# FFN operands made name by name in the text's order, with two and three plain pairs a layer

## The chip, the cores and the metric

The kernel runs on one core of one Trainium2 chip. The metric is the device time of one execution in microseconds, as the median of the runs shown. Engines are named TensorE (PE, with its weight loads as PEld), VectorE (DVE), ScalarE (ACT), GpSimd (POOL) and SyncE (SP, which only issues loads).

## The reference, cut to what matters

A two-layer trunk of 512 tokens and 1024 channels in float32. Each layer is a token mixer (dilated attention in layer 0, causal pooling in layer 1) followed by a gated FFN of width 2816, each behind an RMS norm and with a residual add:

```python
def rmsnorm(x, g):
    y = x * lax.rsqrt(jnp.mean(x * x, axis=-1, keepdims=True) + RMS_EPS)
    return y * g

def swiglu_ffn(h, w_gate_up, w_down):
    gu = h @ w_gate_up
    gate, up = gu[..., :D_FF], gu[..., D_FF:]
    return (jax.nn.silu(gate) * up) @ w_down

for i in range(DEPTH):                       # DEPTH = 2
    x = x + mixer[i](rmsnorm(x, mixer_norm[i]))
    x = x + swiglu_ffn(rmsnorm(x, ffn_norm[i]), w_gate_up[i], w_down[i])
return rmsnorm(x, final_norm)
```

## The kernel before, in words

Activations lie transposed: eight tiles X[k] of 128 channels by 512 tokens. Every matrix product is done in three TensorE passes, because each float32 operand is split into a high part (rounded, by ScalarE) and a low part (the rest, by VectorE): weight high by data high, weight high by data low, weight low by data high. The helper `split` does that for any tile.

**The FFN.** Its 2816 hidden channels are 22 tiles of 128; a pair j is the gate and the up column of one tile. There are two ways to compute a pair.

- A plain pair is two products of 8 x 3 matmuls of 512 columns, made from X scaled by the norm's weights only (`scaled`, the tiles `held[op, k]`). The norm's factor per token (`row`) is not yet needed; VectorE multiplies the result by `row` later. The first pairs of a layer are plain, and they run while the norm is still being computed. Their weights are "lean": ScalarE writes the high part and its negative, and a DMA issued by GpSimd adds the weights from memory to the negative, so VectorE has no part in it.
- A block pair (`strassen_pair`, `chained`) multiplies 2 x 2 blocks by the Strassen-Winograd scheme: seven block products of 4 x 3 matmuls of 256 columns. They are called, in the order of the code, 11, 1, 2, 21, 3, 22, 4. Each name needs an operand T[name, k] from the normed X: sums and differences of its quarters, split into high and low. Three accumulators in PSUM are used several times: alpha takes 11, 2, 3, 4, gamma takes 1 and 22, beta takes 21. Between two uses of an accumulator ScalarE copies it out (lines 535, 539, 543, 551), and the next block product of that accumulator adds on top. The weights of a block pair are made in four steps, `blocks`, `sums`, `more`, `last` (weight tiles b, s, m, l); b serves 11 and 21, s serves 1 and 3, m serves 2 and 22, l serves 4.

Before, `NPLAIN = 4`: four plain pairs in each layer, and `prepare(k)` makes all names of one k beside each of them (line 1108). PARTS says how the hidden tiles are used: pairs 0 and 1 go into plain down products, 2 to 17 into two runs of block down products, 18 to 21 into plain ones.

**The norm ahead of the FFN.** `note` scales a finished X tile and adds its square to a sum. `rstd` sums over channels on TensorE (line 411), VectorE adds epsilon (414), GpSimd raises to -1/2 (417); `spread` brings the result into a row on TensorE (424), ScalarE copies it (430). Before, two products run on seven of eight k ahead of this, the third product is cut in half around `spread`, and five products follow the row.

**The order of work.** The program is written once in text. A scheduler then orders each engine's instructions by the text's priority and by what it takes to be ready, and puts the semaphores. Weights come through rings of five 1024-wide tiles (`w`), two half-wide ones and four raw ones; `pump` is called behind every product and does the next load or weight step when its ring slot is free. `after` in `chained` is a table of hooks: functions that are run in the text behind block product 0 to 6. PSUM has eight banks. Scaled tiles, names, hidden tiles and temporaries share slots: NEAR and SLOTS lie in two large tiles, OPEN are loose.

The steps of a block product, its copy and its hooks:

```python
        mult(alpha, wb, 0, T, "11", n)
        nc.scalar.copy(a, alpha)
        behind(0)
        mult(gamma, ws, 0, T, "1", n)
        nc.scalar.copy(d, gamma)
        behind(1)
        mult(alpha, wm, 0, T, "2", n, on=True)
```

Of the kernel before, what the change touches and what calls it, by code (L numbers as in the profile page):

```python
# [8 lines left out]
F32 = mybir.dt.float32  # L9
F32R = mybir.dt.float32r  # L10
AF = mybir.ActivationFunctionType
OP = mybir.AluOpType
# [38 lines left out]
NEAR = 11  # L51
OPEN = 2
FIXED = NEAR + OPEN
# [12 lines left out]
def trunk(ctx: ExitStack, tc: tile.TileContext, xT, xN, norms, w_first, w_qk, w_qkp, w_v0, w_v0p, w_v12, w_out, w_outp, w_pair, w_down, w_dblock, w_pin, w_pgrp,  # L66
# [134 lines left out]

    turn = [0]

    def pump(n=1, must=False):

        turn[0] += not must
        for i in range(n):
            while loads and all(free(r, c) for r, c in loads[0][1].items()):
                loads[0][0].issued = turn[0]
                loads.popleft()[2]()  # L210
            if not steps or not free(steps[0][1]):
                assert not must
                return
            unit, back = steps[0][0], BACK.get(steps[0][2].__name__)
            if not must and back and unit.back and turn[0] < unit.issued + back:
                return
            steps.popleft()[2]()

    def pairs(*srcs, shift=LINE // 4, back=False):
# [39 lines left out]
    def ffn_plan(layer):  # L259
        j = 0  # L260
        for i, (first, end, block) in enumerate(PARTS):
            while j < min(max(end + block, NPLAIN), FC):
                if j < NPLAIN:
                    plain_gu(layer, j)
                else:
                    pairs(w_pair[layer, j], shift=0, back=True)
                j += 1
            if block:
# [32 lines left out]
    class Product:  # L301


        def __init__(self, n, ins, w=None, keep=None):
            self.n, self.ins, self.done, self.p, self.w = n, ins, 0, ps(), w
            self.sizes = units_of(n)
            self.tiles, self.keep = keep or [], keep is not None
# [10 lines left out]
        def add(self, ks, cols=slice(0, S), pos=None):  # L318
            for k in ks:
                if self.w:  # L320
                    w, c = self.w, k if pos is None else pos + k
                else:
                    held, c = self.where(k)
                    w = held.t
                    if c == self.sizes[len(self.tiles) - 1] - 1 and not self.keep:
                        held.done()
# [52 lines left out]

    def square(layer, k, engine=None):  # L380
        sq = tmp.tile([P, S], F32, name="sq", bufs=3)
        nc.scalar.activation(sq, X[k], AF.Square)
        if layer in acc:
            (engine or nc.vector).tensor_add(sq, acc[layer], sq)
        acc[layer] = sq

    def scaled(layer, k, hi, lo, on_dve=False):
# [7 lines left out]
        operand[layer, k] = hi, lo  # L395

    def note(layer, k):

        if layer < 4:
            held[layer, k], t = slot("h", open=layer == 2 and k == KC - 1)  # L400
            scaled(layer, k, t[:, 0], t[:, 1])
        square(layer, k)
# [197 lines left out]
    with tc.tile_pool(name="opool", bufs=1) as opool:  # L600
        early = [opool.tile([P, 2, S], F32R, tag=f"o{k}", name="early") for k in range(K2)]
        with tc.tile_pool(name="apool", bufs=1) as apool:
# [285 lines left out]
            def halve(h):  # L888

                if h < 3:  # L890
                    OP2[h] = tuple(apool.tile([P, S], F32R, tag=f"qk{h}{c}", name="oh") for c in range(2))
                else:
                    held["o", h], b = slot("oh", open=h == 3)
                    OP2[h] = b[:, 0], b[:, 1]
                split(*OP2[h], o[h])
# [155 lines left out]

            def residual(m, p):
                x = X[m].rearrange("p (q c r) -> p q c r", c=NT, r=NT)
                nc.vector.tensor_add(x, x, p.rearrange("p (r c q) -> p q c r", r=NT, c=NT))
                note(1, m)

            for m in range(NOUT):
                residual(m, lead.pop(0).add([last]).p)
            for u in range(2):
                one, two = (apool.tile([P, S], F32, tag=tag, name="one") for tag in ("s0", "s12"))  # L1060
                seven(T2, one, two, scratch)
                if u:
                    for k in range(2):
                        give(("s", k))
                for c, p in enumerate((one, two)):
                    residual(NOUT + 2 * u + c, p)
# [3 lines left out]
            residual(KC - 1, f.p)  # L1070

    with tc.tile_pool(name="fpool", bufs=2) as fpool:
# [13 lines left out]
        def ffn(layer, nxt, lead, row):  # L1086
# [3 lines left out]
            def gu():  # L1090
                return lead.pop(0).p if lead else product(op)

            def plain_pair(j, up):
                pg = gu()
                gt = ftile("gt")
                nc.vector.tensor_mul(gt, pg, row)
                prepare(j)
                pu = gu()
                if j == NPLAIN - 1:
                    for k in range(KC):  # L1100
                        give((op, k))
                nc.vector.tensor_mul(up, pu, row)
                nc.scalar.activation(gt, gt, AF.Silu)
                nc.vector.tensor_mul(up, up, gt)

            T = {}

            def prepare(k):


                h, t = normed(op, k, row, Temp(), Temp(), True)
                hq, b22 = h.t.rearrange("p (a b c) -> p a b c", a=2, b=2), h.t[:, 3 * H2:]
                held["t", k, 0], b = slot("tb", apart=True)
                split(b[:, 0].rearrange("p (a c) -> p a c", a=2), b[:, 1].rearrange("p (a c) -> p a c", a=2), hq[:, :, 0])
                T["11", k], T["21", k] = (tuple(b[:, e, i * H2:(i + 1) * H2] for e in range(2)) for i in range(2))
                for i, names in enumerate((("1", "2"), ("3", "4"))):
                    held["t", k, 1 + i], b = slot("tt", apart=True)
                    split(b[:, 0], b[:, 1], t.t[:, i * S:(i + 1) * S])
                    for a, name in enumerate(names):
                        T[name, k] = tuple(b[:, e, a * H2:(a + 1) * H2] for e in range(2))  # L1120
                if k % 2 == 0:
                    held["t", k, 3], T["n"] = slot("tn", apart=True)
                n = tuple(T["n"][:, e, k % 2 * H2:(k % 2 + 1) * H2] for e in range(2))
                split_neg(*n, b22)
                T["22", k] = n
                h.done()
                t.done()

            B, U, late = {}, {}, deque()

# [43 lines left out]
            def strassen_pair(u, first=None, right=None):  # L1174
                gt = ftile("gt")
                hooks = waiting()
                if "keep" in U:
# [7 lines left out]
                if first:  # L1185
                    hooks.setdefault(2, []).extend([later(give, ("t", k, 1)) for k in range(K2)] + [first])
                if right:
# [8 lines left out]
            def gate_up(j, ahead):  # L1196
                first, block = next((p[0], p[2]) for p in PARTS if p[0] <= j < p[1])
                u = tmp.tile([P, S], F32, tag="sq", name="u", bufs=3) if block or ahead else ftile("up")
                i, odd = (j - first) // 2, j % 2
                if j < NPLAIN:  # L1200
                    plain_pair(j, u)
                elif block and odd and j == FC - 1:
                    strassen_pair(u, later(operands, i, U["even"]), later(operands_right, i, u))
# [7 lines left out]
                elif not block:  # L1211
                    if NPLAIN <= j < FC - 1:
                        U["keep"] = j, u
# [13 lines left out]

            j = 0
            for first, end, block in PARTS:
                while j < min(max(end + block, NPLAIN), FC):  # L1230
                    gate_up(j, block and j == end)
                    j += 1
                last = end == FC
# [28 lines left out]

        lead = begin(2, 1, range(KC - 1))
        row = finish(lead, 1, [KC - 1])
        ffn(0, 2, lead, row)
# [11 lines left out]
        lead = begin(2, 2, range(KC - 2))  # L1277
        row = finish(lead, 2, range(KC - 2, KC))
        Y = {}
# [38 lines left out]
        def mix(g):  # L1318
            if g not in M:
                mixed(g)  # L1320
            for c, f in enumerate(M.pop(g)):
                m = 2 * g + c
                nc.vector.scalar_tensor_tensor(X[m], f.p, nrm[:, 5, m:m + 1], X[m],
                                               op0=OP.mult, op1=OP.add)
                held[3, m], t = slot("n")
                scaled(3, m, t[:, 0], t[:, 1])
            for c in range(2):
                square(3, 2 * g + c)
                give(("y", g, c))

        pool(3)
# [7 lines left out]
        mix(1)  # L1339
        lead = begin(2, 3, range(4, KC))  # L1340
        mix(0)
        for key in [key for key in held if key[0] == "wg"]:
            give(key)
        for f in lead:
            f.add(range(2, 4))
        row = finish(lead, 3, range(2))
        hidden, HALF = ffn(1, 4, lead, row)


# [177 lines left out]
```

## Time and profile before

| what | value |
|---|---|
| median of 3 runs | 1186.02 us (1185.07 to 1186.65) |
| span of the profiled execution | 1184.0 us |
| what lies between that span and the median | 2.0 us |
| TensorE busy in the span | 1175.4 us (99%) |
| VectorE busy | 989.0 us (84%) |
| ScalarE busy | 721.7 us (61%) |
| GpSimd busy | 171.3 us (14%) |

The span runs from the first to the last instruction of one execution on the chip. An engine's busy time leaves out its waits. TensorE's matmuls overlap one another, so the distance between the starts of two matmuls, not the length of one, is what a matmul costs. The first FFN's norm ends at about 482 us of the span, the second one's at about 864.

### The profile page before, as it was taken

The numbers are of one execution on the slowest core, as the hardware profiler recorded it, in microseconds if no ns is written. First come the engines' busy times: TensorE is split into PE (matmuls) and PEld (weight loads), VectorE is DVE, ScalarE is ACT, GpSimd is POOL, SyncE is SP. The second block draws the span as 40 slices with busy tenths as digits, with TensorE's granted clock in tenths as the row PEclk, the third lists the DMA queues.
The fourth block names the chain that finished last, engine by engine and source line by source line (L and its number), as shares of the span: only waits on it lengthen the run. The fifth ranks groups of instructions, "written<-read, shape, count | busy, mean of one in ns | idle before, by whom it ended". The sixth has DMA issues, their size and how long they took to land.

```text
span 1184.0 us, 25180 instructions
## 1 busy us (share of the span) xinstructions
PE 1175.4 (99%) x10042; PEld 1119.9 (95%) x10042; DVE 989.0 (84%) x1733; ACT 721.7 (61%) x1262; POOL 171.3 (14%) x165
## 2 busy tenths in 40 slices
PE   9999999999999999999999999999999999999997
PEld 7889999999999989889999999988889999999997
DVE  7997898889789888699988988656789998898875
ACT  6554564546455557747756775775575766676553
POOL 1101111111111002311111111122130111111100
PEclk9999999999999999999999999999999999999999
DMA  8537667666856557957777877798595777877732
GB/s 302 130 95 187 147 153 166 168 160 152 192 140 169 145 157 195 246 113 203 191 188 189 204 184 209 195 265 208 121 195 119 187 199 195 198 191 193 197 92 72
DMA packets 83766, 207.57 MB, mean 175 GB/s; under 512 B 7856, under 2 KB 13120, under 8 KB 83648
## 3 DMA queue, kind: packets, MB, share of 16 engines
q1 hardware_dynamic: 52672, 144.84, 36.9%
q0 software_dynamic: 30688, 60.83, 31.6%
q8 instruction: 78, 1.28, 0.4%
q14 instruction: 40, 0.33, 0.1%
q10 hardware_dynamic: 288, 0.29, 0.1%
HBM read 203.84 MB, written 2.10 MB: 174 GB/s over the span
## 4 chain that ended last, share of the span: by engine, by line
PE 96%; DMA 1%; issue 1%; DVE 1%; ACT 0%; POOL 0%; POOLq 0%; DVEq 0%; ACTq 0%
PE ps L461 21%; PE ps L462 20%; PE ps L463 20%; PE ps L329 7%; PE ps L330 7%; PE ps L332 7%; PE ps L928 2%; PE ps L632 2%; PE ps L633 2%; PE ps L634 2%; DMA raw<-w_outp 1%; PE ps L847 1%; PE ps L716 1%; PE ps L736 1%; PE ps L841 1%
## 5 line engine op out<-in xcount | busy, mean ns | idle before, releaser
L92 ACT ACTIVATE w<-raw 128x1024 fp32r<-128x1024 f32 x268 | 283.7, 1063 | 177.0 <-PE ps L463 73.3
L93 DVE TENSOR_TENSOR w<-raw,w 128x1024 fp32r<-128x1024 f32 x268 | 326.4, 1222 | 48.8 <-ACT w L92 44.7
L461 PE MATMUL ps<-far,w 128*128 128x256 f32 x896 | 246.5, 275 | 0.0
L462 PE MATMUL ps<-far,w 128*128 128x256 f32 x896 | 246.4, 275 | 0.0
L463 PE MATMUL ps<-far,w 128*128 128x256 f32 x896 | 246.4, 275 | 0.0
L461 PE MATMUL ps<-near,w 128*128 128x256 f32 x676 | 190.5, 282 | 0.0
L462 PE MATMUL ps<-near,w 128*128 128x256 f32 x676 | 186.9, 277 | 0.0
L463 PE MATMUL ps<-near,w 128*128 128x256 f32 x676 | 186.9, 276 | 0.0
L462 PEld LDWEIGHTS ps<-far,w 128*128 128x128 f32 x896 | 168.2, 188 | 0.1
L461 PEld LDWEIGHTS ps<-far,w 128*128 128x128 f32 x896 | 168.2, 188 | 0.1
L463 PEld LDWEIGHTS ps<-far,w 128*128 128x128 f32 x896 | 168.2, 188 | 0.0
L461 PEld LDWEIGHTS ps<-near,w 128*128 128x128 f32 x676 | 127.1, 188 | 0.5
L462 PEld LDWEIGHTS ps<-near,w 128*128 128x128 f32 x676 | 127.1, 188 | 0.0
L463 PEld LDWEIGHTS ps<-near,w 128*128 128x128 f32 x676 | 127.0, 188 | 0.0
L329 PE MATMUL ps<-near,w 128*128 128x512 f32 (+1 forms) x316 | 119.4, 379 | 0.0
L332 PE MATMUL ps<-near,w 128*128 128x512 f32 (+1 forms) x316 | 118.7, 376 | 0.0
L330 PE MATMUL ps<-near,w 128*128 128x512 f32 (+1 forms) x316 | 118.7, 376 | 0.0
L173 POOL DMA_DIRECT2D raw<-w_pair x36 | 43.6, 1210 | 291.7 <-DMA raw<-w_pair 87.3
L329 PEld LDWEIGHTS ps<-near,w 128*128 128x128 f32 x316 | 59.3, 188 | 11.0 <-ACT near L92 0.4
L332 PEld LDWEIGHTS ps<-near,w 128*128 128x128 f32 x316 | 59.3, 188 | 10.9
L330 PEld LDWEIGHTS ps<-near,w 128*128 128x128 f32 x316 | 59.4, 188 | 10.6 <-DVE near L93 0.2
L92 ACT ACTIVATE half<-rawhalf 128x512 fp32r<-128x512 f32 x84 | 52.8, 630 | 13.7 <-PE ps L463 11.8
(333 smaller groups left out, 2802.7 us busy)
## 6 DMA issues: line engine op xcount, KB each, us to landing
raw<-w_pair SPq DMA_DIRECT2D x80, 512.0 KB, 4.9
raw<-w_qkp SPq DMA_DIRECT2D x38, 512.0 KB, 4.5
raw<-w_pair POOLq DMA_DIRECT2D x36, 512.0 KB, 7.6
raw<-w_dblock SPq DMA_DIRECT2D x32, 512.0 KB, 4.7
raw<-w_qkp POOLq DMA_DIRECT2D x19, 512.0 KB, 7.5
raw<-w_v SPq DMA_DIRECT2D x18, 512.0 KB, 4.1
rawhalf<-w_pair SPq DMA_DIRECT2D x36, 256.0 KB, 5.2
raw<-w_dblock POOLq DMA_DIRECT2D x16, 512.0 KB, 7.5
```

The source lines that it names most:

```text
L92: nc.scalar.activation(hi, v, AF.Copy)
L93: nc.vector.tensor_tensor(lo, v, hi.bitcast(F32), op=OP.subtract)
L173: nc.gpsimd.dma_start(self.b.rearrange("p (a c) -> p a c", a=2), self.src[:, None, 3 * n:].to_broadcast([P, 2, n]), accum_op=OP.add)
L329: nc.tensor.matmul(self.p[:, cols], w[0][:, s], mh[:, cols], start=self.done == 0, stop=False)
L330: nc.tensor.matmul(self.p[:, cols], w[0][:, s], ml[:, cols], start=False, stop=False)
L332: nc.tensor.matmul(self.p[:, cols], w[1][:, s], mh[:, cols], start=False, stop=self.done == self.n)
L461: nc.tensor.matmul(dst, w.t[0][:, c], th, start=k == 0 and not on, stop=False, skip_group_check=on)
L462: nc.tensor.matmul(dst, w.t[0][:, c], tl, start=False, stop=False, skip_group_check=on)
L463: nc.tensor.matmul(dst, w.t[1][:, c], th, start=False, stop=k == n - 1, skip_group_check=on)
L632: nc.tensor.matmul(o, mh, wh, start=k == 0, stop=False)
L633: nc.tensor.matmul(o, mh, wl, start=False, stop=False)
L634: nc.tensor.matmul(o, ml, wh, start=False, stop=k == K2 - 1)
```

## The change

- `NPLAIN = (2, 3)`: two plain pairs in layer 0, three in layer 1. Pairs 2 and 3 (layer 0) and 3 (layer 1) are block pairs now. The down weights of the first part come behind two block pairs (AHEAD).
- The names of the block pairs are made one name at a time for all k, in five stages of the generator `prepared`. The stages are written between the plain products, and the last (name 4) behind the first block product.
- `until` makes weight steps at fixed places of the text; `hold` and `barred` keep `pump` from making others there.
- The plain results are left in PSUM. They are scaled, gated and split in the hooks of the first block pair (`scaled_next`, `kept`), not beside their products; Silu works in place on PSUM.
- `finish` takes the norm's sum earlier: in layer 0 half a product stands ahead of it and half between the sum and `spread`; three products follow. In layer 1 two products stand around it, and four follow.
- The last X tiles ahead of the norm are scaled after their squares, not before.
- From the last attention block product pair (layer 0) or the last pooling group (layer 1) to the end of the second block pair VectorE and ScalarE run in the order of the text (`tc.manual_schedule(engines=BY_HAND)`).
- NEAR goes from 11 to 9, OPEN from 2 to 4; a product gives its weights back when all its columns were used, in any order.

The diff, cut to its core:

```diff
-NPLAIN = 4
+NPLAIN = (2, 3)
+AHEAD = 2
+BY_HAND = {mybir.EngineType.DVE, mybir.EngineType.Activation}
-NEAR = 11
-OPEN = 2
+NEAR = 9
+OPEN = 4
...
-            if not steps or not free(steps[0][1]):
+            if not steps or not free(steps[0][1]) or ((hold[0] or steps[0][0] in barred) and not must):
...
+    def until(what):
+        done = False
+        while not done:
+            while loads and all(free(r, c) for r, c in loads[0][1].items()):
+                loads[0][0].issued = turn[0]
+                loads.popleft()[2]()
...
+            unit, ring, f = steps.popleft()
+            done = what in (f.__name__, unit)
+            f()
...
-    def finish(lead, layer, ks):
-        for f in lead:
-            f.add(ks)
+    def finish(lead, layer, now, behind, rest=()):
+        for f, ks in now:
+            f.add(ks)
+        hold[0] = bool(behind)
         r = rstd([acc[layer]])
-        lead += begin(1, layer, range(4))
+        for f, ks in behind:
+            f.add(ks)
+        if behind:
+            until(barred[layer // 2])
+            if layer == 1:
+                until("blocks")
+        else:
+            lead += begin(1, layer, range(4))
+            rest = [(lead[-1], range(4, KC))]
         row = row_of(spread(r))
-        lead[-1].add(range(4, KC))
+        for f, ks in rest:
+            f.add(ks)
...
+            grown(KC - 1, f.p)
+            noted(1, KC - 3)
+            square(1, KC - 1)
+            for k in (KC - 2, KC - 1):
+                noted(1, k)
...
+            def scaled_pair(j):
+                gt, pu = gu(), gu()
+                up = tmp.tile([P, S], F32, tag="sq", name="u", bufs=3) if j > 1 else ftile("up")
+                nc.vector.tensor_mul(gt, gt, row)
                 nc.vector.tensor_mul(up, pu, row)
                 nc.scalar.activation(gt, gt, AF.Silu)
...
+                normed(0)
+                each(lambda p: named("11", p, a(p, 0)))
+                each(lambda p: nc.vector.tensor_sub(a(p, 0), a(p, 1), a(p, 0)))
+                each(lambda p: named("1", p, a(p, 0)))
+                yield
+                normed(1)
+                each(lambda p: nc.vector.tensor_sub(a(p, 0), a(p, 0), d(p, 1)))
+                each(lambda p: named("2", p, a(p, 0)))
+                yield
+                each(lambda p: named("21", p, d(p, 0)))
+                each(lambda p: nc.vector.tensor_sub(a(p, 1), d(p, 1), a(p, 1)))
+                each(lambda p: named("3", p, a(p, 1)))
+                yield
+                each(lambda p: named("22", p, d(p, 1), split_neg))
+                yield
+                each(lambda p: nc.vector.scalar_tensor_tensor(d(p, 0), a(p, 0), -1.0, d(p, 0), op0=OP.mult, op1=OP.subtract))
+                each(lambda p: named("4", p, d(p, 0)))
...
+            next(stage)
+            upto(2 * plains - 2)
+            until("sums")
+            upto(2 * plains - 1)
+            next(stage)
+            until("more")
+            next(stage)
+            until("last")
+            upto(2 * plains)
+            until("blocks")
+            next(stage)
...
+            j = plains
+            beginning.update({0: [lambda: next(stage)], 1: [later(until, "sums")], 2: [scaled_next] * (plains - 2),
+                              3: [later(until, "more"), scaled_next], 4: [scaled_next], 5: [kept], 6: [free_again]})
...
+                    if j == plains + 1:
+                        ordered.__exit__(None, None, None)
...
-        lead = begin(2, 1, range(KC - 1))
-        row = finish(lead, 1, [KC - 1])
+        lead = begin(1, 1, range(K2))
+        row = finish(lead, 1, [], [(lead[0], range(K2, KC))], [])
+        lead += begin(1, 1, range(KC))
...
         lead = begin(2, 3, range(4, KC))
+        ordered = tc.manual_schedule(engines=BY_HAND)
+        ordered.__enter__()
         mix(0)
...
-        row = finish(lead, 3, range(2))
+        row = finish(lead, 3, [(f, range(2, 4)) for f in lead], [(lead[0], range(2)), (lead[1], range(1))], [(lead[1], range(1, 2))])
```

More of the change, by code (lines that the diff above doesn't have):

```diff
@@ L1090, in gu @@
             def gu():
[L1091 to L1101, printed above, removed]
+                return lead.pop(0).p
+            def scaled_pair(j):
+                gt, pu = gu(), gu()
+                up = tmp.tile([P, S], F32, tag="sq", name="u", bufs=3) if j > 1 else ftile("up")
+                nc.vector.tensor_mul(gt, gt, row)
@@ L1102, in plain_pair, with gated @@
                 nc.vector.tensor_mul(up, pu, row)
                 nc.scalar.activation(gt, gt, AF.Silu)
+                return gt, up
+            def gated(gt, up):
                 nc.vector.tensor_mul(up, up, gt)
             T = {}
[L1108 to L1127, printed above, removed]
@@ L1185, in strassen_pair @@
                 if first:
-                    hooks.setdefault(2, []).extend([later(give, ("t", k, 1)) for k in range(K2)] + [first])
+                    hooks.setdefault(2, []).extend([later(give, ("t", name, p)) for name in "12" for p in range(2)] + [first])
                 if right:
```

111 lines of the change are left out of this document (85 added, 26 removed).

## The prediction

> **What bounds the kernel now.** I read the page first, then the waits of TensorE, then stretches of the timeline around the first FFN.
>
> ```profile
> span 1184.0 us, 25180 instructions
> PE 1175.4 (99%) x10042; PEld 1119.9 (95%) x10042; DVE 989.0 (84%) x1733; ACT 721.7 (61%) x1262; POOL 171.3 (14%) x165
> PEclk9999999999999999999999999999999999999999
> ```
> ```profile
> PE ps L908 <- DVE idle L905: 1.2, 1, 1.2
> PE ps L841 <- ACT t L808: 0.8, 1, 0.8
> ```
>
> TensorE is the bound: busy 99%, and it waited twice in the whole run, 2.0 us together. So time falls only if TensorE gets less work, and rises by whatever it newly waits. The stretches around the first FFN show what stands close behind it (columns: length, then the engine's busy time):
>
> ```profile
> 482.70:500.00 17.30, 17.30 (x78) 14.28 (x77) 17.27 (x31) 15.01 (x22) 5.57 (x6) 1.00 1.04 224
> 500.00:523.00 23.00, 23.00 (x104) 19.10 (x103) 22.86 (x39) 9.64 (x17) 3.03 (x3) 1.00 0.78 148
> 523.00:561.00 38.00, 38.00 (x337) 38.00 (x336) 33.97 (x62) 26.67 (x47) 4.66 (x4) 1.00 0.63 164
> ```
>
> For 40 us after the norm VectorE (third busy figure) is as full as TensorE; later it is at 89%. It has no room exactly where the change works.
>
> **The gain: TensorE's work.** Three plain pairs become block pairs (two in layer 0, one in layer 1).
>
> ```profile
> 490.02 0.39 PE L329 MATMUL ps<-near,w 128*128 128x512 f32 x1
> ...
> 495.46 0.39 PE L329 MATMUL ps<-near,w 128*128 128x512 f32 x1
> ```
> ```profile
> 543.36 0.37 ACT L535 COPY first<-ps 128x256 f32<-128x256 f32 x1 [0.26 <-PE ps L463]
> ...
> 552.88 0.37 ACT L535 COPY first<-ps 128x256 f32<-128x256 f32 x1 [0.26 <-PE ps L463]
> ```
>
> The two matmuls are 24 apart: a product of 24 takes 5.44 us, 0.227 each, a plain pair of two products 10.9. The same copy of two successive block pairs is 9.52 us apart: 84 matmuls, 1.36 per block product of 12. A conversion saves 10.9 - 9.52 = 1.37, three 4.1 us. This is the whole gain.
>
> **What VectorE pays.** Its queue and ScalarE's give the prices, read from start to start:
>
> ```profile
> 478.23 0.16 DVE L414 TENSOR_SCALAR var<-ps 128x4 f32<-128x4 f32 x1 [4.80 <-PE ps L411]
> ...
> 482.66 0.69 DVE L1096 TENSOR_TENSOR gt<-ps,row 128x512 f32<-128x512 f32 x1 [4.27 <-ACT row L430]
> 483.26 1.41 DVE L578 SCALAR_TENSOR_TENSOR temp<-x,nrm,row 128x512 f32<-128x512 f32 x2
> 484.58 0.69 DVE L1102 TENSOR_TENSOR up<-ps,row 128x512 f32<-128x512 f32 x1
> 485.19 0.68 DVE L582 TENSOR_TENSOR temp<-temp 128x512 f32<-128x512 f32 x1
> ...
> 524.01 1.23 DVE L93 TENSOR_TENSOR w<-raw,w 128x1024 fp32r<-128x1024 f32 x1
> 525.15 0.42 DVE L93 TENSOR_TENSOR near<-t,near 128x256 fp32r<-128x256 f32 x1
> 525.49 0.42 DVE L97 SCALAR_TENSOR_TENSOR near<-u,near 128x256 fp32r<-128x256 f32 x1
> ```
> ```profile
> 482.03 0.60 ACT L430 ACTIVATE row<-ps 128x512 f32<-128x512 f32 x1 [0.98 <-PE ps L424]
> ...
> 485.26 1.05 ACT L146 ACTIVATE w<-raw 128x1024 fp32r<-128x1024 f32 x1
> 486.21 0.62 ACT L92 ACTIVATE far<-temp 128x512 fp32r<-128x512 f32 x1
> 486.73 1.05 ACT L147 ACTIVATE w<-w 128x1024 fp32r<-128x1024 f32 x1
> ```
> ```profile
> 477.78 0.36 PE ps L411 x32
> ...
> 481.10 0.89 PE ps L424 x8
> ```
>
> VectorE: 0.60 for 512 columns, 0.66 for a norm product, 1.14 for a 1024-wide weight split, 0.34 for 256. ScalarE: 0.52 (visible after 0.62), 0.95 (1.06), a copy of 256 columns 0.37. A handoff is about 0.05 (row ends 482.63, VectorE starts 482.66). A plain pair costs VectorE 3 x 0.60 = 1.8 (its weights go by ScalarE and DMA); a block pair three splits of 1.14, two adds and a half split of 0.60, five 256-wide steps: 6.9. So each conversion adds 5.1 us to the engine without room and takes 1.4 us away under which it could hide.
>
> The clock below starts (t = 0) when the row is spread on TensorE (481.99 in this trace); VectorE gets the row at 0.67. Operands cost the same as before: 8 norm products, 8 subtractions, 14 splits, 8 x 0.66 + 6 x 0.60 + 2 x 0.66 + 12 x 0.60 + 2 x 0.66 = 18.7 us. What changes is the time under them. Before, the first block pair began 40 us after the row. After, in layer 0 three products are left (16.35) and the pair starts.
>
> **Layer 0, in the text's order.** VectorE: four norm products to 3.3; names 11 to 4.7; subtractions to 5.9; name 1 to 7.3; the pair's sums split, behind ScalarE's half, to 8.8; norm products to 11.5; subtractions 12.7; name 2 14.1; two adds 15.3; the third split must wait for ScalarE's half (1.06) and ends 17.6; name 21 18.9; subtractions 20.1. ScalarE then has, in this order, name 3's second half (20.2), the half split, the next pair's block split, name 22 twice (23.2), and only then the copy of block product 11 out of its bank, done 23.6. Block product 2 adds into that bank, so it cannot start before 23.7. TensorE is there at 16.35 + 2 x 1.36 = 19.1: a wait of 4.6, or 3.2 if 21 is moved ahead.
>
> The second wait is behind the copy of 2 + 3 (line 551), which the text puts behind hook 3: beta's add (29.7), two adds (30.9), ScalarE's half of the next weights (31.0 to 32.05), VectorE's (33.2), the first scaled product (33.8), its Silu (34.5), then the copy, done 34.9. Block product 4 starts there and ends at 36.3. Without waits the pair would end at 16.35 + 9.52 = 25.9: 10.4 late. The second pair's product 2 then waits 2.0 for a copy queued behind the two hidden-tile splits and a Silu (41.0), and two small waits make it 13.1. With TensorE's own order free (21 and the next pair's 11 in front) I get 11.9; with all handoffs and drain times at zero 9.0. I take 11.
>
> **Layer 1.** Four products and a bit (22.5) follow the row, so the first copy is in time (24.8 against 25.2). But six unread products and two accumulators fill the eight PSUM banks; beta gets one when VectorE has scaled the first pair (31.7), where 21 was due at 26.5, and product 4 waits for the same chain of hook 3 until 39.0. In the text's order 11.0, with TensorE's order free 9.8, without handoffs 6.7. I take 9.
>
> **Bounds.** Even if every name were early, hook 3 alone puts 1.2 + 1.06 + 1.14 + 0.60 + 0.62 + 0.37, some 5 us, between the end of 21 and product 4, where TensorE has 2.7 of own work, and the first pair's hooks hold 12.4 us of VectorE work in 9.5 (name 4 2.5, sums 1.1, adds and split 2.3, two scalings 2.4, gating and hidden splits 2.4, own steps 1.7): some 4 a layer is the least in this reading. Above: 13.1 + 11.0, and 0 to 3 for the down weights, whose split now lies in the second pair and which land late:
>
> ```profile
> w<-w_down POOLq DMA_DIRECT2D x8, 512.0 KB, 8.7
> ```
>
> **What I cost at nothing.** Ahead of the row only half a product (12 matmuls, 2.7 us) stands between the last attention product and the norm's sum; add, square and add take 0.69 + 0.62 + 0.69 = 2.0 and handoffs. It just covers; uncovered it costs up to 0.5. From sum to spread 12 matmuls (layer 0) or 9 (layer 1, 2.0 us) cover this:
>
> ```profile
> 478.47 1.39 POOL L417 TENSOR_TENSOR rcol<-var,nhalf 128x2 f32<-128x2 f32 x2 [5.08 <-DVE var L414]
> ```
>
> From the variance at 478.23 to its end at 479.86 are 1.6 us: covered in both, with 0.3 at risk in layer 1. The last plain weights and (layer 0) the next blocks' split now stand on ScalarE ahead of the row, 2 x 0.95 + 0.95 under the 4 us that are left of 2.7 + 0.4 + 2.7 + 0.9 after the sum's adds; in layer 1 the last weights may hold the row up 0.5. On the queues a conversion removes three SP loads, three accumulating DMAs of POOL (the scaling negative copy plus weights in memory) and four ScalarE passes of 0.95, and adds three SP loads, one accumulating DMA and 3.4 us of ScalarE splits; SP keeps its order. The DMA share stood at 1.04 in the first stretch above, so a late load is possible; its price is one landing, the 8.7 above, less what is left under it, and I count it in the upper bound alone. Smaller slots, the count of used columns and the pool mixer's two late scalings add no instruction.
>
> **The clock.** TensorE's only long idle time here is the end:
>
> ```profile
> 1176.00:1184.00 8.00, 1.65 (x43) 1.23 (x41) 2.85 (x7) 1.62 (x3) 1.05 (x2) 0.88 0.55 198
> ```
>
> There the granted clock fell to 0.88 over 8 us, 1.0 us of clock lost. If each of four waits does that, 4 us come on top. The Trainium skill (TensorE: Matmul & The Clock Gate, "What's actually happening") says the clock is halved after an idle window of about 3.4 us and comes back after as long a busy one; by it each such wait would cost an estimated 1.7 more, 6.8 in all. The last row agrees in kind; no run here shows the return.
>
> **Sum.** 1184.0 - 4.1 + 11 + 9 = 1199.9 of span. The median of the runs is 1186.02, 2.0 above this span, so 1201.9.
>
> **The rivals.**
> - The timetable holds (the other sign): TensorE finds other block products whenever a copy is late, or the compiled order lets the copies pass. For it: the names are finished within 2 to 3 us of their use (22 at 24.8, due 23.2), and the scheduler did move work before: a scaling (484.58) ran ahead of a subtraction (485.19) that the text puts first. Against it: VectorE and ScalarE are now bound to the text, and the bank count leaves at most one block product to bring forward. Time: 1186.0 - 4.1 = 1181.9; it decides while the new waits are under 1.7 us together. Chance 0.20.
> - The waits nearly cancel the gain: 1.7 to 6.5 us together, within 0.2% (2.4 us, about what a measurement of this kernel can tell from no change), around 1186. It needs the copies on time and only hook 3 late. Chance 0.12.
> - The waits are long and the clock falls with them: 1201.9 + 4 = 1206, up to 1213 with the upper bounds. Chance 0.08.
> - My forecast, waits of 8 to 27 us: 1190 to 1209, chance 0.60.
>
> **How the numbers follow.** Slower 0.60 + 0.08 = 0.68, same 0.12, faster 0.20. The likeliest case has its own range 1190 to 1209 (1186 - 4.1 + 8, and 1186 - 4.1 + 27). To leave out no more than 2 in 10 the range reaches down to the first rival: 1181.5 to 1209.
>
> **What would show it.** Matmuls of 512 columns fall by 144 and those of 256 rise by 252: the gain. In the waits of TensorE new rows on the block products' lines (461 to 463 here), released by ScalarE's copies (lines 535, 543, 551) or, in layer 1, by VectorE's scaling; each FFN's start holds all of them. Copies start later than their block products' ends by several us there and by 0.2 later on. VectorE without gaps from the row to the second pair. I am wrong if TensorE's waits stay near 2 us, if they sit at the norm's sum or on weights, or if copies run ahead of the splits that stand before them in the text.

## The result and the profile after

The changed kernel takes 1224.64 us (1223.76 to 1225.15, four runs) against 1185.98 (1185.07 to 1186.65) beside it: a ratio of 1.0324, 95% interval 1.0310 to 1.0339. It is slower, as forecast, but by 38.7 us where the forecast had 15.9, and above the range.

The page of the profile after: its span, the busy times and TensorE's granted clock.

```profile
span 1222.0 us, 25401 instructions
PE 1188.6 (97%) x10150; PEld 1134.2 (93%) x10150; DVE 1004.1 (82%) x1745; ACT 720.5 (59%) x1270; POOL 168.6 (14%) x159
PEclk9999999999999999889999999999998999999999
```

The clock dips in two places, the two FFN starts. The count of matmuls is 108 above that of before, as 144 fewer of 512 columns and 252 more of 256 make it. The waits of TensorE, where before had two (columns: tile and line, releaser; us in total, times, longest):

```profile
PE ps L350 <- DMA w<-w_down: 11.2, 3, 6.1
PE ps L499 <- DVE up L1149: 6.0, 3, 3.3
PE ps L499 <- ACT first L573: 3.0, 3, 1.8
PE ps L499 <- ACT w L94: 2.0, 1, 2.0
PE ps L499 <- ACT sums L577: 1.6, 1, 1.6
PE ps L501 <- DVE w L95: 0.8, 1, 0.8
```

Lines 499 to 501 (461 to 463 before) are the block products, 573 to 589 (535 to 551 before) their copies, L94 and L95 `split`, L1149 the scaling of a plain result. The rows on the block products are what the forecast spoke of, 14.2 us with two small ones not shown. The first row is what it nearly left out, the weights of the plain down products; waits "on weights" were among its own signs of being wrong. Stretches of 2 us show what stands behind the waits (length, TensorE's busy time, granted clock, share of the DMA engines, GB/s):

```profile
498.00:500.00 2.00, 2.00 (x12) 0.50 0.17 59
526.00:528.00 2.00, 0.81 (x2) 0.50 1.13 217
528.00:530.00 2.00, 2.00 (x10) 0.50 0.89 282
```

In the first row TensorE counts as busy and does less work: 12 matmuls touch these 2 us, where 0.113 us from start to start would make 17 or 18. Between 440 and 1000 us, taken by 1 us windows, its idle time is 25.5 us and the clock lost while it was busy another 11.8; before had 0.0 of both.

**Where the 38 us are.** From start to start, at full clock, two matmuls of 256 columns lie 0.113 us apart and two of 512 lie 0.227 apart. What the distances have above that, waits and slow clock together, comes to 12.9 us in layer 0 from the row to the second pair and 8.5 around the first down products; in layer 1 to 10.2 and 7.4. With small waits at 961 to 979 us (1.4) that is 40.4. Less the gain of 4.1 it makes 36.3 of the 38.0 by which the spans differ; 1.7 is not placed.

### The profile page after: what moved, and what is told of

It is laid out like the page before. It is cut to its first block, busy times and chain, and to the rows that moved or that the text cites. A ratio compares the mean times of both kernels' runs of the same rounds, so it can differ in the third digit from the quotient of the medians.

```text
span 1222.0 us, 25401 instructions
## 1 busy us (share of the span) xinstructions
PE 1188.6 (97%) x10150; PEld 1134.2 (93%) x10150; DVE 1004.1 (82%) x1745; ACT 720.5 (59%) x1270; POOL 168.6 (14%) x159
## 4 chain that ended last, share of the span: by engine, by line
PE 84%; DVE 6%; DMA 4%; ACT 3%; issue 2%; POOL 0%; DVEq 0%; POOLq 0%; ACTq 0%
PE ps L499 19%; PE ps L501 19%; PE ps L500 19%; PE ps L347 5%; PE ps L350 5%; PE ps L348 5%; PE ps L966 2%; PE ps L670 2%; PE ps L672 2%; PE ps L671 2%; DMA raw<-w_pair 1%; DMA w<-w_down 1%; DVE w L95 1%; DMA raw<-w_outp 1%; ACT w L94 1%
## 5 line engine op out<-in xcount | busy, mean ns | idle before, releaser
L94 ACT ACTIVATE w<-raw 128x1024 fp32r<-128x1024 f32 x277 | 292.0, 1061 | 199.6 <-PE ps L501 69.6
L95 DVE TENSOR_TENSOR w<-raw,w 128x1024 fp32r<-128x1024 f32 x277 | 336.9, 1221 | 64.7 <-ACT w L94 61.1
L499 PE MATMUL ps<-far,w 128*128 128x256 f32 x968 | 270.6, 280 | 13.2 <-DVE up L1149 6.0
L501 PE MATMUL ps<-far,w 128*128 128x256 f32 x968 | 268.7, 278 | 0.8 <-DVE w L95 0.8
L500 PE MATMUL ps<-far,w 128*128 128x256 f32 x968 | 269.2, 278 | 0.0
L499 PEld LDWEIGHTS ps<-far,w 128*128 128x128 f32 x968 | 184.5, 191 | 15.5 <-DVE up L1149 6.6
L501 PEld LDWEIGHTS ps<-far,w 128*128 128x128 f32 x968 | 184.3, 191 | 1.0 <-DVE w L95 1.0
L500 PEld LDWEIGHTS ps<-far,w 128*128 128x128 f32 x968 | 184.6, 191 | 0.2
L499 PE MATMUL ps<-near,w 128*128 128x256 f32 x558 | 158.0, 283 | 0.1
L500 PE MATMUL ps<-near,w 128*128 128x256 f32 x558 | 154.3, 277 | 0.0
L501 PE MATMUL ps<-near,w 128*128 128x256 f32 x558 | 154.2, 276 | 0.0
L499 PEld LDWEIGHTS ps<-near,w 128*128 128x128 f32 x558 | 104.9, 188 | 0.8 <-ACT first L573 0.3
L500 PEld LDWEIGHTS ps<-near,w 128*128 128x128 f32 x558 | 105.0, 188 | 0.0
L501 PEld LDWEIGHTS ps<-near,w 128*128 128x128 f32 x558 | 104.9, 188 | 0.0
L350 PE MATMUL ps<-near,w 128*128 128x512 f32 (+1 forms) x248 | 93.5, 379 | 11.2 <-DMA w<-w_down 11.2
L175 POOL DMA_DIRECT2D raw<-w_pair x39 | 47.0, 1205 | 354.8 <-DMA raw<-w_pair 92.1
L347 PE MATMUL ps<-near,w 128*128 128x512 f32 (+1 forms) x248 | 93.6, 379 | 0.0
L348 PE MATMUL ps<-near,w 128*128 128x512 f32 (+1 forms) x248 | 93.0, 375 | 0.0
L350 PEld LDWEIGHTS ps<-near,w 128*128 128x128 f32 x248 | 47.2, 191 | 20.5 <-DMA w<-w_down 12.2
L94 ACT ACTIVATE half<-rawhalf 128x512 fp32r<-128x512 f32 x87 | 54.6, 629 | 11.9 <-PE ps L501 10.1
L191 DVE TENSOR_TENSOR raw<-raw 128x512 f32<-128x512 f32 x87 | 59.4, 683 | 0.7 <-DVE qk L554 0.4
L192 DVE TENSOR_TENSOR raw<-raw 128x512 f32<-128x512 f32 x87 | 59.4, 682 | 0.3
```

Of the source, the lines that this page charges most:

```text
L94: nc.scalar.activation(hi, v, AF.Copy)
L95: nc.vector.tensor_tensor(lo, v, hi.bitcast(F32), op=OP.subtract)
L175: nc.gpsimd.dma_start(self.b.rearrange("p (a c) -> p a c", a=2), self.src[:, None, 3 * n:].to_broadcast([P, 2, n]), accum_op=OP.add)
L191: nc.vector.tensor_add(a[:, :n], a[:, :n], b[:, :n])
L192: nc.vector.tensor_add(a[:, n:], a[:, n:], a[:, :n])
L347: nc.tensor.matmul(self.p[:, cols], w[0][:, s], mh[:, cols], start=self.done == 0, stop=False)
```

## The experiments

Three theories stand against each other. Q: the fixed order of VectorE and ScalarE puts the copies late. D: the down weights, which take two passes of ScalarE and then a DMA that adds, come late by themselves. V, the rival: VectorE has too much to do in any order, so the waits only move.

**Order free.** The three places that enter or leave the fixed order are taken out.

```diff
-                    ordered = tc.manual_schedule(engines=BY_HAND)
-                    ordered.__enter__()
...
-                        ordered.__exit__(None, None, None)
```

> The changed kernel (1224.6 us) without the text's order: the scheduler orders VectorE and ScalarE as before. Theory Q (queue order: copies are late because the text puts splits ahead of them): the 14 us of waits at copies, banks and weights shrink to under 5 and with them some 5 us of half clock; the down weights' 12.8 us stay: about 1208 to 1212. Rival V (VectorE has too much work at the start, whatever its order): the waits only move, 1220 to 1229. Rival D (down weights and clock are the larger half): no statement beyond Q or V, but the waits on the down weights stay at 10 us or more.

1207.41 us, ratio 1.0178 (1.0163 to 1.0193): 17.2 us come back. Its waits of TensorE:

```profile
PE ps L350 <- DMA w<-w_down: 15.5, 4, 6.1
PE ps L452 <- POOL rcol L445: 0.8, 1, 0.8
```

The long waits on copies and scalings are gone, and those on the down weights have grown by 4.3. The time is just under the range of theory Q and far from V's.

**Down weights by VectorE.** The halves of the first plain down products are made by `split`, with no DMA that adds.

```diff
-lean=layer == 0 or first == 0,
+lean=layer == 0 and first > 0,
```

> The changed kernel with the first part's down weights split by VectorE from the loaded tile, in place of the accumulating DMA: two splits of 1.14 us a layer more on VectorE, no landing of 9 us. Theory D (the down products wait for that DMA, and the clock falls behind the wait): the waits of 11 us on the down weights go, with some 4 us of half clock, against up to 2 us for VectorE: 1208 to 1213. Theory V alone (VectorE is the bound there): the wait comes back as waits on VectorE, 1220 to 1227.

1206.56 us, 1.0169 (1.0154 to 1.0184): 18.1 us come back, and the other half of the table stays:

```profile
PE ps L499 <- DVE up L1149: 6.0, 3, 3.3
PE ps L499 <- ACT w L94: 2.0, 1, 2.0
PE ps L499 <- ACT first L573: 1.7, 1, 1.7
```

More came back than the waits of 11.2 us on these weights: the half clock behind them goes too (6.2 us of clock lost instead of 11.8). The time is below the range given by 1.4.

**TensorE kept busy.** Twenty-four matmuls of 512 columns, whose result is not used, stand ahead of the first down products of each layer.

```diff
+                        spare = ps()
+                        for i in range(24):
+                            nc.tensor.matmul(spare, act[0][0][:, :P], act[0][0], start=True, stop=True)
```

> The changed kernel with 24 useless matmuls of 512 columns (5.4 us) ahead of the first down products of each layer, so that TensorE is busy while it would wait for the down weights. If the clock falls because TensorE is idle (theory C): the fill lies inside the wait of 6.1 and 4.6 us, and the half clock behind it (some 2.2 us in layer 0, 1.5 in layer 1) goes: 2 to 4 us faster, 1221 to 1223. If the low clock is tied to anything else (the rival): no gain, or the 10.9 us of added work shows in part, 1225 to 1231.

1223.53 us, 1.0307 (1.0291 to 1.0322). Two times 5.44 us of added work cost nothing; the wait on the down weights falls from 11.2 to 6.3 and the clock lost from 11.8 to 6.7. The intervals overlap with that of the changed kernel, so whether anything was gained stays open; the work fitted into a time that was lost either way.

**Copies early, still by hand.** The hooks of the first block pair are put later, so that the text has the copies ahead of the weight steps and scalings.

```diff
-            until("blocks")
-            next(stage)
...
-beginning.update({0: [lambda: next(stage)], 1: [later(until, "sums")], 2: [scaled_next] * (plains - 2),
-                  3: [later(until, "more"), scaled_next], 4: [scaled_next], 5: [kept], 6: [free_again]})
+beginning.update({1: [lambda: next(stage)], 2: [lambda: next(stage)] + [scaled_next] * (plains - 2),
+                  3: [scaled_next], 4: [later(until, "blocks"), later(until, "sums"), scaled_next],
+                  5: [later(until, "more"), kept], 6: [free_again]})
```

> The changed kernel with the hooks of the first block pair moved so that its copies stand early in the text: name 22 behind block product 1, name 4 behind 2, the next pair's weight steps behind 3 and 22 in place of ahead of the pair and behind 21. Theory Q: the waits inside the first block pair (some 7 us in layer 0, 6 in layer 1, and their half clock) shrink by half or more: 1214 to 1219. Rival V: VectorE has the same work to do by the same point, the waits move into the second block pair: 1222 to 1227.

1227.65 us, 1.0342 (1.0325 to 1.0360). Theory Q's figure is missed. The waits moved into the second block pair, as V had it; the time lies just above V's range, and its interval overlaps with that of the changed kernel:

```profile
PE ps L499 <- ACT first L573: 11.8, 3, 5.3
PE ps L350 <- DMA w<-w_down: 10.4, 2, 6.0
PE ps L499 <- ACT sums L589: 3.9, 2, 2.0
```

What was put behind the copies is itself due soon. In layer 0 the first pair's copies end 21.7 and 28.3 us after the spread instead of 23.7 and 34.8, and product 11's of the second pair still ends at 40.9, where it was 40.8.

**Both.** Free order, and the down weights by VectorE.

> The changed kernel with both edits: the scheduler's order for VectorE and ScalarE, and the first part's down weights split by VectorE. If the text's order and the down weights' DMA are the two causes and the low clock follows from them (theories Q and D together): hardly a wait is left, and the gain of three block pairs shows: 1182 to 1186, clock 0.999. If VectorE's load is a third cause (rival V: 2 x 2.3 us more work, no accumulating DMA to hide it): 1188 to 1196 with new waits on VectorE.

1189.14 us, 1.0027 (1.0018 to 1.0037): 35.5 of the 38.7 us are back, the sum of the two single edits (17.2 + 18.1 = 35.3). Q and D are separate and together nearly the whole cause. The gain of 4.1 us should have given 1182, so some 7 are missing. V's part in them is argued, not shown by an edit. The waits that are left are 1.2 us at the norm's sum, 1.2 at its spread and 1.2 at block products, all in layer 0. At the spread it is GpSimd's queue: the variance was ready at 472.77, but DMA issues stood ahead of the power, which began at 473.83. The rows are stretches of 15 us around layer 0's first block pair, in order the changed kernel (two rows) and the run with both edits (two rows), with the busy times of TensorE, its weight loads, VectorE, ScalarE and GpSimd ahead of clock, DMA share and GB/s:

```profile
490.00:505.00 15.00, 12.27 (x91) 11.87 (x90) 13.31 (x19) 8.39 (x16) 0.00 (x0) 0.89 0.30 86
505.00:520.00 15.00, 10.85 (x65) 10.42 (x65) 9.78 (x18) 10.96 (x19) 2.52 (x2) 0.77 0.57 156
```
```profile
490.00:505.00 15.00, 15.00 (x118) 14.41 (x117) 15.00 (x26) 8.98 (x15) 0.00 (x0) 1.00 0.24 72
505.00:520.00 15.00, 13.78 (x93) 12.43 (x93) 13.65 (x23) 10.36 (x19) 2.46 (x2) 1.00 0.68 152
```

With the order free VectorE has no gap in the first 15 us and 1.35 in the next; bound to the text it stood still for 6.9 of 30 us just where it was short of time. In layer 1 this run shows no wait in the FFN, and still 312.3 us pass from its norm's sum to the final norm's, where 309.3 passed before; 2.7 of that are products that now stand behind the sum, 1.4 are the gain, and 1.65 are lost. The weight loads show how most of it went:

```profile
889.94 0.19 PEld L499 LDWEIGHTS ps<-far,w 128*128 128x128 f32 x1 [0.20 <-ACT first L581]
```

A matmul lasts 0.28 us and the next starts after 0.113, so a wait under 0.17 leaves no idle time on TensorE; it stands in the distances only (1.3 us between 884 and 922).

**The kernel before, with three plain pairs.** No fixed order, no new steps; only `NPLAIN = 3`, the names of k 2 and 3 both beside the third pair.

> The kernel before with three plain pairs a layer in place of four, names made k by k as there (the last two k beside the third pair), the scheduler's order. TensorE's work falls by 2 x 1.37 us. Theory V (VectorE has no room: 30 us of TensorE work for some 35 of VectorE behind the row): waits of 3 to 6 us a layer eat the gain, 1188 to 1195. Theory G (the scheduler finds other work, the gain shows): 1183 to 1184.5.

1195.72 us, 1.0084 (1.0070 to 1.0098). One plain pair less in each layer, two conversions, should gain 2.7 us of work; the run is 9.6 us slower than the kernel before beside it. Its largest wait, VectorE's variance and GpSimd's queue:

```profile
PE ps L424 <- POOL rcol L417: 4.4, 1, 4.4
```
```profile
478.47 0.16 DVE L414 TENSOR_SCALAR var<-ps 128x4 f32<-128x4 f32 x1 [6.25 <-PE ps L411]
483.73 1.20 POOL L173 DMA_DIRECT2D raw<-w_pair  x1 [11.55 <-DMA raw<-w_pair]
484.48 1.88 POOL L417 TENSOR_TENSOR rcol<-var,nhalf 128x2 f32<-128x2 f32 x2
```

The code has the same 12 matmuls between the norm's sum and its spread as before. The variance was ready at 478.63, but in GpSimd's queue the adding load of a block pair stood ahead of the power and waited for another load until 483.73, so the power began at 484.48. The time lies just above V's range (1195), and since this wait is one of GpSimd's order, the run does not price VectorE's load alone.

**Two and two.** The run with both edits, and `NPLAIN = (2, 2)`.

> As the kernel with both edits, with two plain pairs in layer 1 too: 1.37 us less on TensorE than there, but only two products (10.9 us) between the second row and the first block pair, where the names of the first two block products need VectorE for 8 us. If names arrive in time: 1.4 us under that kernel. If layer 1 needs the third product as cover (my guess): 2 to 8 us over it, with waits on VectorE in layer 1 alone.

1191.78 us, 1.0049 (1.0036 to 1.0062), 2.6 above the run with two and three. The fourth conversion loses more than its 1.37 gains: TensorE waits 3.2 us in all on the copies of L573 and L589, against 0.8. That is within the guess of 2 to 8 us more, but 1.2 of the 3.2 stand in layer 0, where no wait was expected.

**VectorE alone by hand, ScalarE alone by hand.** The down weights by VectorE, and one engine in `BY_HAND`.

```diff
-BY_HAND = {mybir.EngineType.DVE, mybir.EngineType.Activation}
+BY_HAND = {mybir.EngineType.DVE}
```

> The changed kernel with the down weights split by VectorE (1206.6 us) and only VectorE in the text's order, ScalarE free. If the copies are late because ScalarE's queue holds splits ahead of them (theory Q as I worked it out): the copies go ahead, half or more of the 12 us of waits and most of the half clock go: 1190 to 1197. If the bound text on VectorE is enough to make TensorE wait (banks and splits in VectorE's order): 1200 to 1207.

> Only ScalarE is bound to the text's order, VectorE is free; the down weights' halves are added by VectorE. The mirror of the run that bound VectorE alone (1209.0 us) beside the one that bound both (1206.6 us) and the one that bound neither (1189.1 us). If VectorE's order is the cause: 1189 to 1194 us. If either order is enough, since each engine waits for the other's halves of the copies and of the conversions: 1200 to 1210 us.

VectorE alone: 1208.97 us, 1.0195 (1.0181 to 1.0209). ScalarE alone: 1190.86 us, 1.0041 (1.0028 to 1.0053). Beside them both bound 1206.56 and neither 1189.14. The run with ScalarE bound lies in the range given for VectorE's order as the cause; that with VectorE bound lies 2 us above both of its ranges. So, with the down weights by VectorE, it is VectorE's order that costs the time, and freeing ScalarE under it brings nothing:

```profile
PE ps L499 <- ACT first L573: 6.8, 5, 3.0
PE ps L499 <- DVE up L1149: 4.4, 2, 3.3
PE ps L439 <- DVE sq L405: 2.1, 1, 2.1
```
```profile
PE ps L499 <- ACT first L573: 2.1, 2, 1.9
PE ps L452 <- POOL rcol L445: 1.5, 1, 1.5
```

The first fence is of VectorE bound, the second of ScalarE bound. Both name a ScalarE copy as the releaser: it is the last link, and says nothing of what held it. The copies of product 11 in the first and the second pair of layer 0, with VectorE alone bound:

```profile
475.77 1.24 PE L452 MATMUL ps<-ident,rcol 128*128 128x128 f32 x8
...
495.50 0.35 ACT L573 COPY first<-ps 128x256 f32<-128x256 f32 x1
...
512.43 0.39 ACT L573 COPY first<-ps 128x256 f32<-128x256 f32 x1
```

From the spread's end they end at 18.8 and 35.8; with neither engine bound at 18.3 and 28.1; with both bound at 23.7 and 40.8.

**By hand up to the row only; three and three.** The fixed order ends at the norm's row in both layers, down weights by VectorE; then the same with a third plain pair in layer 0, without `until("blocks")` ahead of the row.

```diff
+        ordered.__exit__(None, None, None)
         ffn(0, 2, lead, row)
```

> VectorE and ScalarE are bound to the text's order only from the last residual additions to the norm's row; from there on the order is free, and the down weights' halves are added by VectorE, as in the run with free order at 1189.1 us. That run's first norm sum began at 472.1 us after a wait of 1.2, against 469.3 in the changed kernel, and TensorE waited 1.2 us more for the norm's row. Theory N (the little that the free order still lost lies mostly ahead of the row, where the scheduler lets other work pass the norm): 4 us come back, 1184 to 1187 us. Rival (VectorE has too much to do ahead of block product two in any order; a norm that is earlier only leaves less of it done): 1188 to 1192 us, with longer waits on the copies.

> As the run that binds the two engines up to the row alone, with three plain pairs in layer 0 too (three and three), and without the step that makes block product one's last operands ahead of the row in layer 0. One conversion more, 1.4 us, and some 14 us more of TensorE work ahead of block product two in layer 0. Theory: the 1 to 2 us of waits at that product go, so 0 to 1.5 us above or below the run with two and three, 1183 to 1187 us. Rival (the steps of the name-by-name making keep VectorE late whatever stands ahead): 1188 to 1192 us.

Up to the row: 1187.83 us, 1.0018 (1.0010 to 1.0027). 1.3 us came back, not 4, and the intervals of the two runs overlap, so even that is open. The norm's sum starts at 470.8 instead of 472.1, and then the wait is at the copies (`sums` L589, 1.5 us). Neither theory's range holds it, V's reason is the nearer. From the row VectorE has no gap at all:

```profile
475.00:490.00 15.00, 15.00 (x68) 12.40 (x68) 15.00 (x24) 7.44 (x13) 0.37 (x1) 1.00 0.59 133
490.00:505.00 15.00, 14.90 (x124) 14.47 (x123) 15.00 (x24) 10.28 (x18) 0.00 (x0) 1.00 0.27 83
```

Three and three: 1195.28 us, 1.0079 (1.0066 to 1.0093), above the rival's range too. The wait is not at product two but at the norm again (3.9 us on GpSimd's power, and the half clock behind it):

```profile
474.02 0.15 DVE L442 TENSOR_SCALAR var<-ps 128x4 f32<-128x4 f32 x1
476.74 1.25 POOL L175 DMA_DIRECT2D raw<-w_pair  x1
477.49 1.92 POOL L445 TENSOR_TENSOR rcol<-var,nhalf 128x2 f32<-128x2 f32 x2
```

The norm's sum starts later (473.1), and the power begins 3.3 us after the variance is ready, because DMA issues follow one another in GpSimd's queue ahead of it. So this run tests neither theory.

No version beat the kernel before; the nearest, by hand up to the row, is 0.18% slower.

## Why the prediction was right or wrong

**The direction and the main mechanism were right.** The forecast followed VectorE's and ScalarE's text from the row and had product 11's copy done 23.6 us after the spread, so begun at 23.2; the copy of 2 + 3 done at 34.9; the second pair's at 41.0. The chain of work shows the spread's end at 473.58, then ScalarE's timeline the copies:

```profile
472.67 0.91 PE ps L452 x8
473.58 0.02 issue
```
```profile
496.91 0.35 ACT L573 COPY first<-ps 128x256 f32<-128x256 f32 x1
...
507.98 0.38 ACT L589 COPY sums<-ps 128x256 f32<-128x256 f32 x1
514.02 0.35 ACT L573 COPY first<-ps 128x256 f32<-128x256 f32 x1
```

They end at 23.7, 34.8 and 40.8. With the order known, the queue could be worked out to 0.2 us over 40. TensorE lost 12.9 us there in layer 0 where 11 was said (9.0 to 13.1), and 10.2 in layer 1 where 9 was said (6.7 to 11.0): 23.1 against 20. The free order took the long waits away. The make-up is not the forecast's: of the 23.1 only 12.8 is idle time, the rest is half clock and slow restarts, which it had not put into the 20. And in layer 0 the longest of these waits, 2.3 us, was released by the scaling of a plain result, which it had expected in layer 1 alone.

**The detail on ScalarE was one link only.** The forecast put the copy behind name 3, the half split, the next block split and name 22 in ScalarE's queue. With that queue free and VectorE bound the first pair's copy did come 4.9 us earlier (18.8 against 23.7), but TensorE waited at the second pair's instead, and the time did not fall (1208.97 against 1206.56). The queue that decides the time is VectorE's.

**The step that failed is the down weights.** The forecast said of a late load "its price is one landing, the 8.7 above, less what is left under it, and I count it in the upper bound alone", and gave the down weights 0 to 3 us. It was 15.9 us from start to start, 11.2 of it plain waiting; the edit that takes it away brought 18.1. The rows of ScalarE, of GpSimd and of the chain of work that ended last:

```profile
515.05 1.07 ACT L148 ACTIVATE w<-raw 128x1024 fp32r<-128x1024 f32 x1
...
516.32 1.05 ACT L149 ACTIVATE w<-w 128x1024 fp32r<-128x1024 f32 x1
```
```profile
517.86 9.28 DMA w<-w_down
527.19 0.80 PE ps L350
```
```profile
517.86 1.31 POOL L151 DMA_DIRECT2D w<-w_down  x1 [8.49 <-ACT near L94]
...
527.48 1.31 POOL L151 DMA_DIRECT2D w<-w_down  x1 [5.16 <-issue]
```

Two passes of ScalarE (the second ends at 517.37), an issue and a landing of 9.28 follow one another, and TensorE takes the weights 0.05 after they land. The forecast had the landing, 8.7, and saw that the split lay in the second pair. It did not ask what is left under it: only the second pair, some 9.5 us, stands ahead of the down product, and ScalarE's part begins when that pair is under way: TensorE was there at 521.1, the weights at 527.1. Two such places at the price of one landing each are 17.4 us. The reading was at hand and not done. It would not have needed the order to slip: with the order free the wait is longer (15.5), since TensorE then comes sooner.

**The clock was a rival and is a part.** The forecast gave the case of long waits with a falling clock 4 us and a chance of 0.08, from 1.0 us lost at the end of the trace. The clock was lost six times, 11.8 us, some 2.0 each. The Trainium skill (TensorE: Matmul & The Clock Gate, "What's actually happening") states a half-rate clock after an idle window of about 3.4 us and full rate after as long a busy one. The halving and the stretches of half clock, 3.41 us or twice that here, agree. A wait need not be that long: the clock fell after waits of 1.83 us and more. The 1.7 each that the forecast worked out by that page were nearer than the 1.0 taken from the trace. Stretches of 3.41 us, first of the changed kernel, then two of the free order (length, TensorE's busy time, granted clock, share of the DMA engines, GB/s):

```profile
494.16:497.57 3.41, 0.80 (x4) 1.00 0.27 68
497.57:500.98 3.41, 3.41 (x18) 0.50 0.17 56
500.98:504.39 3.41, 3.41 (x32) 1.00 0.00 0
511.22:514.63 3.41, 1.58 (x13) 1.00 0.71 121
514.63:518.04 3.41, 3.41 (x17) 0.50 0.27 72
```
```profile
912.15:915.56 3.41, 1.51 (x12) 1.00 0.94 146
915.56:918.97 3.41, 3.00 (x13) 1.00 0.91 131
```

In the changed kernel the six stretches of half clock begin at 497.57, 507.81, 514.63, 524.87, 917.41 and 937.89, whole multiples of 3.41 us apart, and ahead of each stands a stretch of 3.41 us in which TensorE was busy for 1.58 us or less. So in these traces a fall goes with how idle such a stretch was, not with the length of a wait alone. In the free order a wait of 2.31 us, spread over the two stretches of the second fence, left the clock at 1.00, and so did one of 1.97 in the run with TensorE kept busy. The busy time at which the clock falls is not settled: 1.58 went with a fall, 1.51 did not.

The loss lies in the 23.1 and the 15.9 above, so it isn't added again.

**What was costed at nothing held in the changed kernel.** No wait at the norm's sum or its spread appears in its table. The run with both edits waited 1.2 at the sum and 1.2 at the spread. The fixed order is not a sure guard: with it the runs with the down weights by VectorE, with TensorE kept busy and with the copies early waited 1.1, 1.1 and 1.8 at the spread. So that it held here was in part luck.

**The sum, corrected.** 1184.0 - 4.1 + 23.1 + 15.9 + 1.4 = 1220.3, and 1222.0 was measured. The rival on the other side, a timetable that holds (1181.9), did not come with a free order either: with it and the down weights by VectorE, VectorE is full from the row on, and the gain is spent (1187.8 at best).

## What to carry to other kernels

Where work is moved from an engine with slack onto one without, follow that engine's queue in the order it will really have. And for each weight or operand ask in the same way what stands between its first step and its use: if the chain of passes and one DMA landing is longer than the work under it, the difference is a wait, not an upper bound. Waits on the bound engine can cost more than their length: price the long ones with the half clock behind them. And ask the same of an engine with little to do: GpSimd's one small step of the norm came late whenever DMA issues stood ahead of it in its queue.

## What the runs showed of the hardware that was not expected

- In the changed kernel the granted clock fell to 0.50 with each of the six waits of 1.8 us or more, for 3.41 or 6.83 us; waits of 1.6 us and less left it at 1.00. It is no rule of the length: in other runs waits of 1.97 and 2.31 us left it at 1.00 as well.
- GpSimd's second adding DMA for the down weights was issued at 527.48, 0.34 after the first had landed, though nothing that the profile shows held it for the last 5.16 us. In layer 1 the same pair of issues shows 6.00. Whether the queue takes only so many adding DMAs at a time was not tried; in the kernel before GpSimd issued three, each 6.6 us or more from landing, between 480.57 and 483.25.
- Waits under 0.17 us don't appear as idle time of TensorE, and cost 1.3 us in one stretch; the weight loads' rows show them.
